# A third MLP product done as seven quarter products, fixed tiles for the raw up weights, and a rewritten passage from the up half to the down half

## The chip, the cores and the metric

The kernel runs on one core of a Trainium2 chip. The metric is the device time of one execution in microseconds (us), lower is better. All arithmetic that matters is float32: a matrix product is made of three TensorE passes over operands that were split into a high and a low part (`hi*hi + hi*lo + lo*hi`).

## The reference, cut to what matters

One decoder layer on x of shape (1, 1024, 1024): a first RMS norm, differential attention and a gated delta rule side by side, an output projection, and then the MLP, which is all that the change touches:

```
h = rms_norm(x, norm2_w)
x = x + jnp.square(jax.nn.relu(h @ w_up)) @ w_down      # w_up 1024 x 4096, w_down 4096 x 1024
```

Both products of the MLP are computed with a seven-product (Strassen-like) scheme: the operands are cut into 2 x 2 blocks, seven products of sums and differences of blocks take the place of eight products of blocks, and the blocks of the result are sums of the seven.

## The kernel before, in words

**The up half** (lines 2517 to 2871) makes `relu(h @ w_up)^2`. The 4096 hidden columns are cut into eight groups `g` of 512. In each group there are seven products, numbered 1 to 7. A whole product takes a weight block of 512 inputs x 256 columns and a block of 512 tokens: two column slices of 128 times four input slices times three passes, so 24 matmuls of 512 tokens each (`prod_up`, lines 2414 to 2416). For groups 2 to 7 the *second* product is cut once more: `sixth_second` does it as seven sub-products on quarters, each of two input slices times three passes on 256 tokens, so 42 matmuls of 256 (lines 2657 to 2659). Its results go to halves of the bank `Z` and VectorE adds them to the tile `ua` with `plus` (line 2632).

From group 2 on a group's work is six calls in a row, `sixth_second`, `first`, `third`, `seventh`, `fifth`, `fourth` (lines 2851 to 2862); `first` and `fifth` already do those products for the next group. PSUM holds the banks `X[0]`, `X[1]`, `Y`, `Z`. The raw weights of a group are four tiles `raw` named a, b, c, d, loaded by `load_w` (line 2534) into a pool of eight tiles; `combine` forms their sums and differences on VectorE (line 2568), `rounded` makes the high part on ScalarE (line 2572), `rest` the low part on VectorE (line 2576). The quarters of the weights for the second product are summed on GpSimd (`quarters`, lines 2584 to 2588) in the tile `qf`, which takes the place of tile `s4`, and split into `qs`.

A finished block of hidden values (tiles `ua`, `b`, `c`, `ud`, and the differences `s3`, `s4`) is written to one of seven DRAM buffers `ud1` to `ud7`, one for each product of the down half. `put` notes the transfer, and `flush(n)` issues all but the last `n` lists of noted transfers on SyncE (SP), whose transfers share one queue.

**The down half** (lines 2872 to 2996) does seven products in two passes `kg`, in the order 1, 5, 6, 3, 7, 2, 4. Each product has two halves. That makes 28 halves, numbered here m = 0 to 27, each of 48 matmuls of 512 columns (lines 2943 to 2945). A half needs 1 MB of hidden values (`u_raw(m)`: a load `ur<-ud` into one of the four tiles ur0 to ur3) and 1 MB of weights (`dn_raw`: two loads `dw` of 512 KB), both split into high and low parts by `split4`: casts on ScalarE (line 2293) and differences on VectorE (line 2294). For one half the order is two casts of `ur`, two of `dw`, each followed on VectorE by its difference. Finished banks are added to the accumulators `acc` by `leave` (line 2926).

Before, the tile of half m is `urs[max(m - 1, 0) % 4]`: halves 0 and 1 share ur0, half 3 has ur2, and half 4 is the first that has ur3. The tile ur3 lies in a pool that takes the place of the pools `up0` and `up1` (tiles `b`, `s4`, `ud`, `c`, `s3`), so its first load waits until the last writes out of `b` and `s4` have landed (lines 2963 to 2967).

TensorE's order is as written in the code throughout. From group 2 to the end of `first` of group 7 that of VectorE and ScalarE is as written too (lines 2849 to 2866); after that a scheduler sets it. SP's order is set by the scheduler in both kernels.

Of the kernel before, what the change touches and what calls it, by code (L numbers as in the profile page):

```python
# [9 lines left out]
F32 = mybir.dt.float32  # L10
# [8 lines left out]
P = 128  # L19
# [225 lines left out]
def tile_hymba_layer(  # L245
# [2273 lines left out]
    uctx = ctx.enter_context(ExitStack())  # L2519
    for name, cx, tags in (("ur0", tpctx, []), ("up1", uctx, ["b", "s4"]), ("up0", uctx, ["ud", "c", "s3"])):  # L2520
# [28 lines left out]
    def u_tile(g, n):  # L2549
        tag = f"ua{g % 2}" if n == "a" else "ud" if n == "d" else n  # L2550
        u[g][n] = ups[tag].tile([P, 2, 512], F32, tag=tag, name=tag, bufs=2 if n == "d" else 1)
        return u[g][n]
# [65 lines left out]

    Q_S = {}

    def quarters_w(g):
        raw = w[g]["b"]
        f = ups["s4"].tile([P, 4, 2, P], F32, tag="s4", name="qf", bufs=1)
# [4 lines left out]
        split([t[:, x].rearrange("p s k c -> p (s k c)") for x in range(2)], f.rearrange("p s k c -> p (s k c)"))  # L2628
        Q_S[g] = [[t[:, x, i] for x in range(2)] for i in range(4)]

# [8 lines left out]
    def slot(f, g):  # L2639
        puts.append([])  # L2640
        f(g)
        flush(2)

    def sixth_second(g):

        rest(g, 6)
        if g > 2:
            act2(u_tile(g - 1, "b"), X[(g - 1) % 2])
            put(g - 1, "b", 2)
        sw, o2 = Q_S.pop(g), early.pop((g, 2))  # L2650
        A = [[[x[:, 2 * j:2 * j + 2, i * P:i * P + P] for x in o2] for j in range(2)] for i in range(2)]
        a = u[g]["a"]
        r0, r1, z0, z1 = [Z[i // 2][:, i % 2 * 256:i % 2 * 256 + 256] for i in range(4)]

        def sub(out, wt, xt, start, stop):
            for k in range(2):
                T.matmul(out, wt[0][:, k], xt[0][:, k], start=start and k == 0, stop=False, skip_group_check=True)
                T.matmul(out, wt[0][:, k], xt[1][:, k], start=False, stop=False, skip_group_check=True)
                T.matmul(out, wt[1][:, k], xt[0][:, k], start=False, stop=stop and k == 1, skip_group_check=True)  # L2659

# [3 lines left out]
        plus(a[:, 0, 0:256], r0)  # L2664
        plus(a[:, 0, 0:256], r1)
        sub(z0, A[1][1], Q_T[3], True, True)
        sub(z1, sw[0], Q_T[0], False, False)
        plus(a[:, 1], Z[1])
        if g < NG - 1:
            rounded(g + 1, 1)  # L2670
        for _ in range(2):
# [9 lines left out]
        sub(z1, sw[3], B2[1][1], False, True)  # L2681
        if g < NG - 1:
            rest(g + 1, 1)
        combine(g, 3)
# [5 lines left out]
        rounded(g, 3)  # L2690

    def first(g):
        for _ in triples(g + 1, 1, X[1 - g % 2], True) if g < NG - 1 else ():
            pass
        S.copy(u_tile(g, "c"), X[g % 2])
        rest(g, 3)
        combine(g, 7)
        act2(u[g]["a"])
        put(g, "a", 1)
        rounded(g, 7)  # L2700

    def third(g):
        for _ in triples(g, 3, Y, False, True):
            pass
        S.copy(u_tile(g + 1, "a"), X[1 - g % 2])
        rest(g, 7)
        combine(g + 1, 5)
        rounded(g + 1, 5)

    def seventh(g):  # L2710
        t = u[g]
        for _ in triples(g, 7, X[g % 2]):
# [21 lines left out]
    def fourth(g):  # L2734
        t = u[g]
        for _ in triples(g, 4, X[g % 2], False, True):
            pass
        S.copy(u_tile(g + 1, "d"), Y)
        V.tensor_tensor(t["a"], t["c"], t["a"], ALU.subtract)
# [13 lines left out]
    def product(g, i):  # L2753
# [24 lines left out]
        elif i == 5:  # L2778
            S.copy(u_tile(g, "d"), Y)
        elif i == 6:  # L2780
# [6 lines left out]
        elif i == 7:  # L2787
# [3 lines left out]
            act2(t["d"])  # L2791
            put(g, "d", 4)
            V.tensor_tensor(t["c"], t["c"], t["d"], ALU.add)
# [35 lines left out]
    def loaded_after(g, i):  # L2829
        if i == 7:  # L2830
            load_w(g + 2, "ab")
        elif i == 4:
            load_w(g + 2, "cd")

    for g, i in todo:
        step(g, i)
        if (g, i) == (1, 6):
            quarters_x()
        elif (g, i) == (1, 3):
            sums = quarters_w(2)  # L2840
            next(sums)
        elif (g, i) == (2, 5):
            next(sums, None)
        loaded_after(g, i)
    rounded(2, 2)
    rest(2, 2)
    combine(2, 6)
    rounded(2, 6)
    ordered = ctx.enter_context(ExitStack())
    ordered.enter_context(tc.manual_schedule(engines={V.engine, S.engine}))  # L2850
    for g in range(2, NG - 1):
        slot(sixth_second, g)
        slot(first, g)
        slot(third, g)
        slot(seventh, g)
        sums = quarters_w(g + 1)
        next(sums)
        loaded_after(g, 7)
        slot(fifth, g)
        slot(fourth, g)  # L2860
        next(sums, None)
        loaded_after(g, 4)
    g = NG - 1
    slot(sixth_second, g)
    slot(first, g)
    ordered.close()
    step(g, 3)
    flush(1)
    rest(g, 7)
    step(g, 7)  # L2870
    step(g, 4)
    octx.close()

    ur = ctx.enter_context(tc.tile_pool(name="ur", bufs=1, **right))

# [5 lines left out]
    lo, hi = slice(0, 512), slice(512, 1024)  # L2881
    turn_of = [0]
    for tb in tiles:
        accs[tb] = row_tile("acc")

    ur0 = pools["ur0"].tile([P, 4, 512], F32, tag="ur0", name="ur0")
    urs = [ur0] + [ur.tile([P, 4, 512], F32, name=f"ur{i}") for i in (1, 2)]
    wds = [{} for _ in range(NK)]
# [14 lines left out]
    def u_raw(m):  # L2903
        if m < len(halves):
            kg, i, s = halves[m]
            g0 = 4 * kg + 2 * s
            return nc.sync.dma_start(urs[max(m - 1, 0) % 4].rearrange("p (g q) t -> p g q t", g=2),
                                     ud[i][g0:g0 + 2].rearrange("g p q t -> p g q t"))
# [8 lines left out]

    def down(kg, wd, i, flip, n, out, start, stop):
        bank = bankB if flip ^ (kg % 2) else bankA
# [10 lines left out]
        for s in range(2):  # L2930
            v = views[4 * (turn_of[0] % 2):][:4]
            turn_of[0] += 1
            m = halves.index((kg, i, s))
            raw = urs[max(m - 1, 0) % 4]
            split4(v[0:2], raw)
            split4(v[2:4], wd[n][s])
            u_raw(m + 4 if m else 1)
            seq = [(j, t) for t in (0, 2, 1, 3) for j in range(4)] if final and s else \
                [(j, t) for j in range(4) for t in range(4)]
            for j, t in seq:  # L2940
# [5 lines left out]
                if final and s1:  # L2946
                    leave(t)
        if not final:
            for t in range(4):
                leave(t)  # L2950

    u_raw(0)
    for n in "ab":
        for s in range(2):
            dn_raw(0, n, s)


    load_acc(tiles[:4])
    u_raw(2)
    u_raw(3)  # L2960
    for s in range(2):
# [10 lines left out]
    for kg in range(NK):  # L2972
# [5 lines left out]

        down(kg, wd, 1, 0, "a", (0, lo), True, False)
        both("b", "b", "a")  # L2980
        down(kg, wd, 5, 1, "b", (1, hi), True, False)
        both("b", "d", "b")
        down(kg, wd, 6, 0, "b", (0, hi), False, False)
        down(kg, wd, 3, 1, "d", (0, hi), False, True)
        both("a", "b", "a")
        down(kg, wd, 7, 0, "a", (1, hi), False, False)
        down(kg, wd, 2, 1, "c", (0, lo), True, True)
        if kg + 1 < NK:
            for s in range(2):
                dn_raw(kg + 1, "a", s)  # L2990
        both("b", "c", "b")
        down(kg, wd, 4, 0, "b", (1, lo), False, True)
        if kg + 1 < NK:
            for n in "bdc":
                for s in range(2):
                    dn_raw(kg + 1, n, s)
    manual.close()
# [48 lines left out]
```

## Time and profile before

| | |
|---|---|
| median of the runs before (lowest to highest, 3 runs) | 1190.36 us (1189.79 to 1192.09) |
| the profiled execution's own time | 1190.33 us |
| its span, first to last instruction | 1188.4 us |
| mean granted TensorE clock | 1.000 |
| busy: TensorE, VectorE, ScalarE, GpSimd | 1178.1, 878.1, 621.3, 190.1 us |
| up half from its steady part on, and down half | 666 to 880 us, and 880 to 1185 us |

In the profile's lines, a group names the code line, the engine, the operation and `out<-in` by tile names; buffer numbers are left out, so `ur<-ud` is any load of hidden values. "Idle before" is the engine's wait in front of the instruction, with what ended it. A transfer's "us to landing" runs from its issue on SP to its last byte. Matmuls are pipelined: one of 512 columns lasts 0.39 us from start to end, but the next one starts 0.23 us after it, so TensorE's pace is read from starts.

### The profile page before, as it was taken

Reading aid. Unit: us, or ns where it says so; the run is one execution under the profiler, and the core shown is the slowest. Engines: PE = TensorE matmul, PEld = TensorE weight load, DVE = VectorE, ACT = ScalarE, POOL = GpSimd, SP = SyncE. Lnnn points to the kernel's source line nnn. Section 1 sums busy time; section 2 is a strip of 40 time slices with the busy share of each in tenths; the row PEclk is TensorE's granted clock in tenths of the full one; section 3 lists DMA queues with packets and bytes.
Section 4 is the critical chain, followed back from the end, with each engine's and each line's share of the span. In section 5 each row is a group of like instructions: output and inputs, shape, how many; then the busy total and the mean of one; then the engine's idle time right before and its main releaser. Section 6 shows DMA issues by size and latency. Waiting matters only on the chain.

```text
span 1188.4 us, 17558 instructions
## 1 busy us (share of the span) xinstructions
PE 1178.1 (99%) x6196; PEld 988.8 (83%) x6196; DVE 878.1 (74%) x1648; ACT 621.3 (52%) x1141; POOL 190.1 (16%) x250
## 2 busy tenths in 40 slices
PE   9999999999999999999999999999999999999998
PEld 8988888788888788888888888888888888888887
DVE  7878799667778888886996666656689755786543
ACT  6656646344556765774765445445473333434330
POOL 2314211432222432222120000000000000000000
PEclk9999999999999999999999999999999999999999
DMA  9358644557545586344545444344399555422301
GB/s 355 121 133 197 183 116 98 127 181 209 188 151 171 153 216 162 90 88 152 178 154 186 177 156 160 127 157 177 143 338 379 204 193 213 142 81 96 142 36 71
DMA packets 179617, 196.09 MB, mean 165 GB/s; under 512 B 81529, under 2 KB 134313, under 8 KB 179529
## 3 DMA queue, kind: packets, MB, share of 16 engines
q1 hardware_dynamic: 173688, 181.56, 48.5%
q0 software_dynamic: 5696, 13.41, 3.5%
q8 instruction: 49, 0.80, 0.3%
q14 instruction: 40, 0.32, 0.1%
q10 hardware_dynamic: 144, 0.00, 0.0%
HBM read 132.73 MB, written 62.19 MB: 164 GB/s over the span
## 4 chain that ended last, share of the span: by engine, by line
PE 49%; DVE 1%; issue 0%; DMA 0%; ACT 0%; DVEq 0%
PE X L2416 5%; PE X L2415 5%; PE X L2414 5%; PE X L2943 4%; PE X L2944 4%; PE X L2945 4%; PE Y L2416 2%; PE Y L2415 2%; PE Y L2414 2%; PE Y L2943 2%; PE Z L2943 2%; PE Z L2944 2%; PE Y L2944 2%; PE Y L2945 2%; PE Z L2945 2%; PE Z L2659 1%
## 5 line engine op out<-in xcount | busy, mean ns | idle before, releaser
L2293 ACT CAST hH<-ur 128x1024 fp32r<-128x1024 f32 x56 | 58.6, 1051 | 167.6 <-PE Y L2944 89.4
L2294 DVE TENSOR_TENSOR hL<-ur,hH 128x1024 fp32r<-128x1024 f32 x56 | 68.2, 1222 | 78.1 <-ACT hH L2293 78.0
L2943 PE MATMUL X<-hH 128*128 128x512 f32 x224 | 87.1, 389 | 0.0
L2944 PE MATMUL X<-hL,hH 128*128 128x512 f32 x224 | 87.1, 389 | 0.0
L2945 PE MATMUL X<-hH,hL 128*128 128x512 f32 x224 | 87.1, 389 | 0.0
L2576 DVE TENSOR_TENSOR op<-raw,op 128x1024 fp32r<-128x1024 f32 x43 | 53.3, 1240 | 34.0 <-PE X L2415 25.0
L1228 PE MATMUL ps_dn<-hH,wH 128*128 128x512 f32 x192 | 76.5, 399 | 0.0
L1229 PE MATMUL ps_dn<-hL,wH 128*128 128x512 f32 x192 | 74.9, 390 | 0.0
L1230 PE MATMUL ps_dn<-hH,wL 128*128 128x512 f32 x192 | 74.9, 390 | 0.0
L2294 DVE TENSOR_TENSOR hL<-dw,hH 128x1024 fp32r<-128x1024 f32 x56 | 68.1, 1217 | 0.2 <-ACT hH L2293 0.2
L2572 ACT CAST op<-raw 128x1024 fp32r<-128x1024 f32 x43 | 44.9, 1043 | 38.5 <-PE Z L2659 23.6
L2293 ACT CAST hH<-dw 128x1024 fp32r<-128x1024 f32 x56 | 58.7, 1048 | 9.0 <-PE X L2945 4.4
L1835 ACT ACTIVATE pexp<-pexp,mx,small 128x128 f32<-128x128 f32 (+7 forms) x64 | 55.1, 862 | 12.5 <-DVE mx L1855 12.5
L829 DVE SCALAR_TENSOR_TENSOR cy<-cp,pv,cy 128x512 f32<-128x512 f32 x72 | 52.2, 736 | 9.8 <-ACT cy L826 9.2
L1334 ACT CAST wH<-wraw 128x512 fp32r<-128x512 f32 x66 | 40.5, 614 | 34.5 <-DMA wraw<-in_w_units_dram 18.5
L1713 PE MATMUL ps_qk<-hH,wH 128*128 128x512 f32 x128 | 53.7, 420 | 0.3 <-DVE tq L1628 0.3
L2165 PE MATMUL ps_op<-wH,hH 128*128 128x512 f32 x128 | 53.1, 415 | 0.0
L1336 DVE TENSOR_TENSOR wL<-wraw,wH 128x512 fp32r<-128x512 f32 x60 | 41.0, 683 | 13.4 <-ACT wH L1334 13.1
L1715 PE MATMUL ps_qk<-hH,wL 128*128 128x512 f32 x128 | 50.2, 392 | 0.0
L2167 PE MATMUL ps_op<-wH,hL 128*128 128x512 f32 x128 | 50.2, 392 | 0.0
L1714 PE MATMUL ps_qk<-hL,wH 128*128 128x512 f32 x128 | 50.0, 391 | 0.0
L2166 PE MATMUL ps_op<-wL,hH 128*128 128x512 f32 x128 | 50.0, 390 | 0.0
(449 smaller groups left out, 3512.6 us busy)
## 6 DMA issues: line engine op xcount, KB each, us to landing
ur<-ud SPq DMA_DIRECT2D x28, 1024.0 KB, 4.9
raw<-in_w_up_dram SPq DMA_DIRECT2D x32, 512.0 KB, 4.0
dw<-in_w_down_dram SPq DMA_DIRECT2D x32, 512.0 KB, 6.5
wraw<-in_w_units_dram SPq DMA_DIRECT2D x38, 256.0 KB, 4.1
ud<-ua SPq DMA_DIRECT2D x16, 512.0 KB, 5.9
ud<-s SPq DMA_DIRECT2D x16, 512.0 KB, 3.1
pka<-park_d SPq DMA_DIRECT2D x32, 192.0 KB, 4.1
xt<-in_x_dram SPq DMA_DIRECT2D x8, 512.0 KB, 10.2
```

What stands on the lines that cost most here:

```text
L1228: T.matmul(ps, wh[:, k, cs], hH[:, k, sl], start=(k == 0), stop=False)
L1229: T.matmul(ps, wh[:, k, cs], hL[:, k, sl], start=False, stop=False)
L1230: T.matmul(ps, wl[:, k, cs], hH[:, k, sl], start=False, stop=(k == KB - 1))
L1835: S.activation(e, e, AF.Exp, scale=negq[h][:, 8 * m + tb:8 * m + tb + 1], bias=bi[:, m:m + 1], accum_out=ssum[:, m:m + 1])
L2293: S.copy(dst[0], src)
L2294: V.tensor_tensor(dst[1], src, dst[0].bitcast(F32), ALU.subtract)
L2414: T.matmul(ps, op[0][:, k, cs], h[0][:, k, :], start=start and k == 0, stop=False, skip_group_check=True)
L2415: T.matmul(ps, op[0][:, k, cs], h[1][:, k, :], start=False, stop=False, skip_group_check=True)
L2416: T.matmul(ps, op[1][:, k, cs], h[0][:, k, :], start=False, stop=stop and k == 3, skip_group_check=True)
L2943: T.matmul(bank[t], v[0][:, j, sl], v[2][:, j], start=s0, stop=False, skip_group_check=True)
L2944: T.matmul(bank[t], v[0][:, j, sl], v[3][:, j], start=False, stop=False, skip_group_check=True)
L2945: T.matmul(bank[t], v[1][:, j, sl], v[2][:, j], start=False, stop=s1, skip_group_check=True)
```

## The change

- **Third product in quarters, groups 3 to 7.** `third_quarters` replaces 24 matmuls of 512 by 42 of 256, on halves of `Z` and on `Y`. Weight quarters come from a second `quarters_w(g, True)` (GpSimd sums in the place of tile `s3`, one more cast, one more difference); quarters of the tokens are made once in group 2 (`quarters_x3` on GpSimd, `operand_x3`). VectorE gets four more additions into `c` (`plus` in `third_quarters` and `spread`).
- **Raw weights in six fixed tiles.** `load_w` writes a group's tile into the one that the group before (a, b) or the one before that (c, d) had; the loads of a, b, c, d are issued at four places instead of two. Tile `ud` has one buffer instead of two, and the copy out of `Y` into it moves from `fourth` to `sixth_second`.
- **The passage and the down half.** The last group's third, seventh and fourth product are written out by hand with the first splits of the down half between them (`ready`), and VectorE and ScalarE follow the written order to the end (`ordered.close()` is now last). A half's operands are prepared one half ahead (`upcoming(m + 1)`), and the additions to `acc` are held back by half a product (`behind`). The tile of half m is now `urs[m % 4]`: half 0 has ur0, half 1 ur1, half 2 ur2, and half 3 is the first that has ur3.

The core of the diff (`...` marks what is left out):

```diff
-                t = row_tile("raw").rearrange("p (k c) -> p k c", k=4)
+                back = 1 if n in "ab" else 2
+                t = w[g - back][n] if g - back > 1 else row_tile("raw").rearrange("p (k c) -> p k c", k=4)
...
+    def third_quarters(g):
+        last = g == NG - 1
+        sw, A, c = Q_S3.pop(g), quartered(early.pop((g, 3))), u[g]["c"]
+        r, z = Z[0][:, 0:256], Z[1][:, 0:256]
...
+        sub(r, A[0][0], B3[0][0], True, False)
+        plus(c[:, 0, 0:256], r)
...
+        sub(z, sw[0], Q_T3[0], True, True)
+        if not last:
+            twice()
+        if not last:
+            sub(Y[:, 0, 0:256], A[0][1], B3[1][0], False, True)
+            S.copy(u_tile(g + 1, "a"), X[1 - g % 2])
+        rest(g, 7)
+        sub(r, sw[1], Q_T3[1], False, False)
+        plus(c[:, 0, 256:512], r)
...
+            sub(Y[:, 1, 0:256], A[1][1], Q_T3[3], False, True)
+        sub(Y[:, 0, 256:512], sw[3], B3[1][1], False, True)
...
+        sub(r, sw[2], Q_T3[2], False, True)
...
     def u_raw(m):
...
-            return nc.sync.dma_start(urs[max(m - 1, 0) % 4].rearrange("p (g q) t -> p g q t", g=2),
+            return nc.sync.dma_start(urs[m % 4].rearrange("p (g q) t -> p g q t", g=2),
...
+    def upcoming(m):
+        if 1 < m < len(halves):
+            kg, i, s = halves[m]
+            v = views[4 * (m % 2):][:4]
+            split4(v[0:2], urs[m % 4])
+            split4(v[2:4], wds[kg][NAMES[i]][s])
+            u_raw(m + 4)
...
     flush(0)
     uctx.close()
     pools["uc"] = tpctx.enter_context(tc.tile_pool(name="uc", bufs=1, **left))
     urs.append(pools["uc"].tile([P, 4, 512], F32, name="ur3"))
-    last = u_raw(4)
+    last = u_raw(3)
+    u_raw(5)
     with tc.issue_after(last.ins):
         load_acc(tiles[4:])
```

**SP at the end of the passage.** The issues around the last write `ud3<-s4` stand on SP before as follows (`ud5` is read by halves 2 and 3, `ud6` by 4 and 5, `ud3` by 6 and 7, and `ur0` to `ur3` are the four tiles):

```order
L2907 DMA ur2_9385<-ud5_128 128x2x1024
L2899 DMA dw_9405<-in_w_down_dram 128x2x512 x2
L2899 DMA dw_9408<-in_w_down_dram 128x2x512
L2562 DMA ud4_127<-ud_9167 128x1024
L2907 DMA ur0_9383<-ud6_129 128x2x1024
L2562 DMA ud2_125<-b_9330 128x1024
L2562 DMA ud5_128<-c_9261 128x1024
L2562 DMA ud6_129<-ua1_9061 128x1024
L2907 DMA ur1_9384<-ud3_126 128x2x1024
L2562 DMA ud3_126<-s4_9367 128x1024
L2907 DMA ur2_9385<-ud3_126 128x2x1024
L2907 DMA ur3_9421<-ud6_129 128x2x1024
```

And in the changed kernel, from the load of half 2 on:

```order
L3007 DMA ur2_9552<-ud5_128 128x2x1024
L2999 DMA dw_9576<-in_w_down_dram 128x2x512
L2563 DMA ud5_128<-c_9393 128x1024
L2999 DMA dw_9576<-in_w_down_dram 128x2x512
L3007 DMA ur0_9449<-ud6_129 128x2x1024
L2999 DMA dw_9579<-in_w_down_dram 128x2x512
L2563 DMA ud6_129<-ua1_9157 128x1024
L3007 DMA ur1_9551<-ud6_129 128x2x1024
L2563 DMA ud2_125<-b_9495 128x1024
L2563 DMA ud3_126<-s4_9569 128x1024
L3007 DMA ur2_9552<-ud3_126 128x2x1024
L3007 DMA ur3_9589<-ud5_128 128x2x1024
```

Before, the load that is last here and waits for the write of `s4` brings half 4, and the first row brings half 3. Now the first row brings half 2, and the last one half 3.

**ScalarE in the first halves of the down half.** Before, from the splits of half 1 on (the casts of `ur0` at the top are half 1, those of `ur1` half 2):

```order
L2293 CAST hH_131<-ur0_9383 128x2x512 x2
L2790 COPY b_9330<-X1_7225 128x1024
L2465 ACTIVATE ud_9167<-ud_9167 128x1024
L2466 ACTIVATE ud_9167<-ud_9167 128x1024
L2465 ACTIVATE b_9330<-b_9330 128x1024
L2466 ACTIVATE b_9330<-b_9330 128x1024
L2293 CAST hH_131<-dw_9393 128x2x512
L2293 CAST hH_131<-ur1_9384 128x2x512 x2
```

Now, from the splits of half 0 on (`ur1` is half 1, `ur2` half 2, `ur3` half 3):

```order
L2293 CAST hH_131<-ur0_9449 128x2x512
L2293 CAST hH_131<-dw_9454 128x2x512 x2
L2293 CAST hH_131<-ur1_9551 128x2x512 x2
L2465 ACTIVATE b_9495<-b_9495 128x1024
L2466 ACTIVATE b_9495<-b_9495 128x1024
L2293 CAST hH_131<-ur2_9552 128x2x512 x2
L2293 CAST hH_131<-dw_9512 128x2x512 x2
L2293 CAST hH_131<-ur3_9589 128x2x512 x2
L2293 CAST hH_131<-dw_9515 128x2x512 x2
```

The casts now come two and two, `ur` ahead of `dw`; the last activation of `b`, from which `s4` is made, stands behind the casts of half 1.

**VectorE in the third product of group 3.** Before, from the low part of product 7's weights to the difference `s3`:

```order
L2576 TENSOR_TENSOR op_8224<-raw_7829,op_8223 128x1024
L2568 TENSOR_TENSOR raw_8101<-raw_8101,raw_8103 128x1024
L2632 TENSOR_TENSOR c_8217<-c_8217,Y_6811 128x1024
L2576 TENSOR_TENSOR op_8256<-raw_8101,op_8255 128x1024
L2718 TENSOR_TENSOR s3_8291<-ua1_7983,c_8217 128x1024
```

Now the same stretch, with the low part of the weight quarters (`qs`) ahead:

```order
L2657 TENSOR_TENSOR qs_8144<-qf_8139,qs_8144 128x1024
L2661 TENSOR_TENSOR c_8236<-c_8236,Z0_7290 128x256
L2661 TENSOR_TENSOR c_8236<-c_8236,Z1_7291 128x2x256
L2577 TENSOR_TENSOR op_8245<-raw_7825,op_8244 128x1024
L2661 TENSOR_TENSOR c_8236<-c_8236,Z0_7290 128x256
L2569 TENSOR_TENSOR raw_7600<-raw_7600,raw_7602 128x1024
L2661 TENSOR_TENSOR c_8236<-c_8236,Z0_7290 128x512
L2661 TENSOR_TENSOR c_8236<-c_8236,Y_6811 128x1024
L2577 TENSOR_TENSOR op_8293<-raw_7600,op_8292 128x1024
L2813 TENSOR_TENSOR s3_8336<-ua1_7990,c_8236 128x1024
```

Four additions out of `Z` and the difference of `qs` are new in this stretch.

More of the change, by code (lines that the diff above doesn't have):

```diff
@@ L2642, in slot, with sub, quartered @@
         flush(2)
+    def sub(out, wt, xt, start, stop):
+        for k in range(2):
+            T.matmul(out, wt[0][:, k], xt[0][:, k], start=start and k == 0, stop=False, skip_group_check=True)
+            T.matmul(out, wt[0][:, k], xt[1][:, k], start=False, stop=False, skip_group_check=True)
+            T.matmul(out, wt[1][:, k], xt[0][:, k], start=False, stop=stop and k == 1, skip_group_check=True)
+    def quartered(o):
+        return [[[x[:, 2 * j:2 * j + 2, i * P:i * P + P] for x in o] for j in range(2)] for i in range(2)]
     def sixth_second(g):
         rest(g, 6)
+        last = g == NG - 1
         if g > 2:
@@ L2649, in sixth_second @@
             put(g - 1, "b", 2)
+        S.copy(u_tile(g, "d"), Y)
         sw, o2 = Q_S.pop(g), early.pop((g, 2))
-        A = [[[x[:, 2 * j:2 * j + 2, i * P:i * P + P] for x in o2] for j in range(2)] for i in range(2)]
+        A = quartered(o2)
         a = u[g]["a"]
         r0, r1, z0, z1 = [Z[i // 2][:, i % 2 * 256:i % 2 * 256 + 256] for i in range(4)]
[L2655 to L2659, printed above, removed]
         steps = triples(g, 6, X[g % 2])
@@ L2694, in first @@
             pass
+        if g == NG - 1:
+            for _ in sums_w3.pop():
+                pass
+            S.copy(u_tile(g, "c"), X[g % 2])
+            rounded(g, 7)
+            act2(u[g]["a"])
+            put(g, "a", 1)
+            return
         S.copy(u_tile(g, "c"), X[g % 2])
         rest(g, 3)
+        if g > 2:
+            next(sums_w3[0])
         combine(g, 7)
+        if g > 2:
+            next(sums_w3.pop(), None)
         act2(u[g]["a"])
@@ L2865, in tile_hymba_layer @@
     slot(first, g)
[L2866 to L2874, printed above, removed]
+    slot(third, g)
     bankA = Z + [Y[:, 0], Y[:, 1]]
@@ L2881, in tile_hymba_layer @@
     lo, hi = slice(0, 512), slice(512, 1024)
-    turn_of = [0]
-    for tb in tiles:
-        accs[tb] = row_tile("acc")
     ur0 = pools["ur0"].tile([P, 4, 512], F32, tag="ur0", name="ur0")
-    urs = [ur0] + [ur.tile([P, 4, 512], F32, name=f"ur{i}") for i in (1, 2)]
+    urs = [ur0]
     wds = [{} for _ in range(NK)]
@@ L2916, in split4, with ready, down @@
             split([x[:, j:j + 2] for x in dst], src[:, j:j + 2])
-    def down(kg, wd, i, flip, n, out, start, stop):
+    def ready(s, weights, j):
+        v = views[4 * s:][:4]
+        dst, src = (v[2:4], wds[0]["a"][s]) if weights else (v[0:2], urs[s])
+        split([x[:, j:j + 2] for x in dst], src[:, j:j + 2])
+    def down(kg, i, flip, out, start, stop, then=None):
         bank = bankB if flip ^ (kg % 2) else bankA
```

217 lines of the change are left out of this document (164 added, 53 removed).

## The prediction

> **What bounds the kernel now.** I read the page's busy shares first, then the list of TensorE's waits, then busy time by stage.
>
> ```profile
> PE 1178.1 (99%) x6196; PEld 988.8 (83%) x6196; DVE 878.1 (74%) x1648; ACT 621.3 (52%) x1141; POOL 190.1 (16%) x250
> ```
>
> ```profile
> PE ps_w L567 <- POOL ident masks.py:199: 1.5, 1, 1.5
> ...
> PE ps_r L528 <- ACT dg L523: 0.2, 1, 0.2
> ```
>
> ```profile
> 0.00:603.00 603.00, 596.59 (x3516) 503.02 (x3517) 488.36 (x1277) 361.45 (x877) 166.55 (x224) 1.00 0.58 162
> 603.00:630.00 27.00, 26.92 (x120) 21.95 (x119) 26.64 (x32) 20.88 (x26) 6.19 (x2) 1.00 0.68 225
> ...
> 704.00:742.00 38.00, 38.00 (x191) 32.31 (x190) 24.85 (x26) 19.41 (x21) 2.86 (x4) 1.00 0.44 153
> ...
> 856.00:880.00 24.00, 24.00 (x115) 20.15 (x114) 19.06 (x19) 15.14 (x16) 0.00 (x0) 1.00 0.81 288
> 880.00:1032.00 152.00, 152.00 (x672) 125.91 (x671) 108.83 (x97) 59.89 (x60) 0.00 (x0) 1.00 0.65 242
> ```
>
> The list has eleven waits of TensorE, none of them at a line of the MLP. From 630 us on its busy time equals the stretch. So in everything that the change touches TensorE is the bound, at a granted clock of 1.00: a matmul that goes shortens the kernel by its pace, work on other engines costs nothing while it stays hidden, and a new wait of TensorE costs its full length, since nothing behind it can catch up. There is no wait to win here. Pace is read from starts:
>
> ```profile
> 664.21 0.28 PE L2657 MATMUL Z<-hH,op 128*128 128x256 f32 x1
> ...
> 667.08 0.40 PE L2414 MATMUL X<-T0h,op 128*128 128x512 f32 x1
> ...
> 674.75 0.39 PE L2414 MATMUL X<-hH,op 128*128 128x512 f32 x1
> ...
> 680.19 0.39 PE L2414 MATMUL Y<-hH,op 128*128 128x512 f32 x1
> ```
>
> The first 24 quarter matmuls of the second product take 667.08 - 664.21 = 2.87 us, 119.6 ns each. A whole product's 24 take 680.19 - 674.75 = 5.44 us, 226.7 ns each.
>
> **Third product in quarters.** It removes 24 x 226.7 ns = 5.44 us and adds 42 x 119.6 ns = 5.02 us: 0.42 us less per group, 2.1 us less over groups 3 to 7, all of it on the bound. Between 256 and 512 columns the trace shows no gap worth a term.
>
> What comes with it lies on other engines:
>
> ```profile
> L2632 DVE TENSOR_TENSOR ua<-ua,Z 128x256 f32<-128x256 f32 x24 | 10.1, 421 | 6.1 <-PE Z L2659 5.4
> L2632 DVE TENSOR_TENSOR ua<-ua,Z 128x512 f32<-128x512 f32 x12 | 8.2, 687 | 5.2 <-PE Z L2659 5.2
> L2294 DVE TENSOR_TENSOR qs<-qf,qs 128x1024 fp32r<-128x1024 f32 x6 | 7.3, 1224 | 6.6 <-ACT qs L2293 6.6
> L2584 POOL TENSOR_TENSOR qf<-raw 128x256 f32<-128x256 f32 x6 | 4.6, 764 | 190.5 <-DMA ud<-s 190.5
> L2611 POOL COPY qr<-qr 128x512 f32<-128x512 f32 x2 | 6.2, 3119 | 29.4 <-issue 29.4
> ...
> L2293 ACT CAST hH<-ur 128x1024 fp32r<-128x1024 f32 x56 | 58.6, 1051 | 167.6 <-PE Y L2944 89.4
> ```
>
> VectorE gets, per group, two additions of 256 (0.42 each), two of 512 (0.69 each) and one difference of 1024 (1.22): 3.4 us on top of 24.85 of 38. ScalarE gets a cast of 1.05 us on top of 19.41, GpSimd four sums of 0.76 on top of 2.86. All three have room, so the sum is nought on average. The tight place is the half bank `r`: its second sub-product may start only when `c` has taken the first, and between the two TensorE has 12 quarter matmuls, 1.43 us, against an addition of 0.42; if VectorE has more than 1 us of other work in front there, TensorE waits for the excess. I take 0; the first rival below takes it up. The eight sums of token quarters in group 2 (512 elements on GpSimd) are not in the trace: bounded by 0.76 for half as many elements and by the 3.1 us of a GpSimd copy of that size, nearest to twice 0.76, about 1.5 each and 12 in all. They are needed a whole group, 38 us, later: 0, and still 0 at 3.1 each.
>
> **Six fixed raw tiles, one `ud` tile.** A load now waits for the last reader of the same tile, and on SP later issues queue behind it. Each has at least one call (5.4 us for a whole product) between issue and first use; VectorE is the one to wait, then TensorE. The copy out of `Y` moves to the next call and waits for the write of the tile; `Y` is next written two calls later. I take 0 for these, at most some tenths.
>
> **The passage.** Here a new wait appears. In the changed kernel half 3 is the first in ur3, whose first load waits until the last write of `s4` has landed; before, that was half 4. So the load is needed 48 matmuls, 10.9 us, earlier. How it stood before:
>
> ```profile
> 861.58 0.37 SPq L2907 DMA_DIRECT2D ur<-ud  x1
> ...
> 896.60 0.32 SPq L2562 DMA_DIRECT2D ud<-s  x1
> ```
>
> ```profile
> 863.42 0.38 SPq L2899 DMA_DIRECT2D dw<-in_w_down_dram  x1
> ```
>
> ```profile
> ud<-s SPq DMA_DIRECT2D x1, 512.0 KB, 12.5
> ```
>
> ```profile
> 909.22 0.37 SPq L2907 DMA_DIRECT2D ur<-ud  x1
> ```
>
> ```profile
> ur<-ud SPq DMA_DIRECT2D x1, 1024.0 KB, 5.3
> ```
>
> ```profile
> 863.00:878.00 15.00, 15.00 (x68) 12.38 (x67) 11.86 (x12) 12.62 (x13) 0.00 (x0) 1.00 0.95 334
> 878.00:893.00 15.00, 15.00 (x68) 12.43 (x67) 15.00 (x12) 11.18 (x11) 0.00 (x0) 1.00 1.02 376
> 893.00:909.00 16.00, 16.00 (x72) 13.27 (x71) 15.18 (x14) 5.06 (x5) 0.00 (x0) 1.00 0.92 355
> ```
>
> The transfers are full from 863 to 909 us (share 0.92 to 1.02). The write of `s4`, issued at 896.60, landed 12.5 us later, at 909.1; at 909.22 the first load of ur3 went out and landed 5.3 later, at 914.5. From the issue of half 0 at 861.58 to that landing SP's order counts six `ur` of 1 MB, twelve `dw` and seven writes of 512 KB: 31 units of 512 KB in 47.5 us, 1.53 us each.
>
> In the changed order the stretch up to the landing of `s4` begins with the first `dw` and has five `ur`, twelve `dw`, seven writes: 29 units, 44.4 us. That first `dw` waits for the end of product 6 of group 7, which comes four groups' savings earlier, 1.7 us: 863.42 - 1.7 = 861.7. So `s4` lands at 906.1, and half 3, with 1 MB (half 6) ahead of it in SP's order, as another load had then, at 906.1 + 0.1 + 5.3 = 911.5.
>
> TensorE's first matmul of the down half:
>
> ```profile
> 879.79 0.39 PE L2943 MATMUL Z<-hH 128*128 128x512 f32 x1
> ```
>
> Now 879.79 - 2.1 = 877.7, and half 3 is due three halves of 48 x 226.7 ns = 10.88 later, at 910.3. Its operands after the landing:
>
> ```profile
> 914.57 2.00 ACT L2293 CAST hH<-ur 128x1024 fp32r<-128x1024 f32 x2 [0.83 <-DMA ur<-ud]
> ```
>
> ```profile
> 915.66 2.36 DVE L2294 TENSOR_TENSOR hL<-ur,hH 128x1024 fp32r<-128x1024 f32 x2 [0.45 <-ACT hH L2293]
> ```
>
> The first matmul needs the third cast (two of `ur`, one of `dw`), 2.0 + 1.05 = 3.0 us after the landing, the second one the third difference: 1.1 us behind the first cast's start, then 2.36 for two and 1.2 for the third, 4.6 us. So the second matmul starts at 911.5 + 4.6 = 916.1 in place of 910.55: **TensorE waits 5.5 us** in front of and in half 3. Twenty-four halves follow at TensorE's pace and give none of it back. Nor does it matter if an earlier half is late by a fraction: the landing, not TensorE, sets this end. Halves 0 to 2 come out ready by the same count: half 0 is the 7th unit (861.7 + 7 x 1.53 = 872.4, due 877.7), half 1 is the 14th unit (861.7 + 14 x 1.53 = 883.1, due 888.6), half 2 the 18th (889.2, due 899.5).
>
> The unknown is the pace of the transfers. At the best of the three stretches throughout (376 GB/s against a mean of 355) the 44.4 us become 41.9 and the wait 3.0; at the worst (334) they become 47.2 and the wait 8.3. I take the mean, which is this same stretch with almost the same transfers.
>
> [...]
>
> The rest of the down half (preparing one half ahead, holding back the additions to `acc`, differences of weights earlier) changes no matmul and hides behind a TensorE that never waited there: 0. The end, one addition and a last write behind the last matmul, is the same.
>
> **The sum**, against the profiled execution's 1190.33 us, practically the median of 1190.36: 1190.33 - 2.1 + 5.5 = **1193.7 us**. About 0.2%, 2.4 us, is what a measurement of this kernel can tell from no change; so slower means above 1192.7, faster below 1188.0.
>
> **Rivals.**
>
> *VectorE or GpSimd become late within a group.* For it: 28.3 us of some 37.3 would be taken on VectorE, the order is fixed, and GpSimd's sums now meet it twice per group. One difference that met them took longer:
>
> ```profile
> 708.60 1.22 DVE L2568 TENSOR_TENSOR raw<-raw 128x1024 f32<-128x1024 f32 x1
> ...
> 712.53 1.60 DVE L2576 TENSOR_TENSOR op<-raw,op 128x1024 fp32r<-128x1024 f32 x1 [1.22 <-PE X L2415]
> ```
>
> 1.60 us against 1.22. Against it: that cost TensorE nothing. It decides once VectorE is over 1 us late at `c += r`; half a microsecond per group would be 2.5 us more, 1196.2. [...] Chance 0.10.
>
> *The load of half 3 comes in time.* The other side: it decides at the landing of half 3. If that is 3.4 us earlier (29 units in 41 us, 385 GB/s), the wait shrinks to the 2.1 us saved and the time is that of before; at 5.6 us earlier there is no wait, and the time is 1190.33 - 2.1 = 1188.2. For it: single stretches reached 376, and the mix has fewer `dw` waiting behind a late issue; against it: the mean over 46 us was 355. Chance 0.28, within it 0.09 for under 1188.0 (a slightly larger saving is enough) and 0.19 for no change.
>
> *The forecast*, a wait of 3.5 to 8 us at half 3: chance 0.62; in 0.13 of it the wait is under 4.5 us and the sum within 0.2%, in 0.49 it is slower.
>
> **How the numbers follow.** Slower 0.49 + 0.10 = 0.59, same 0.13 + 0.19 = 0.32, faster 0.09. The forecast's own range is 1191.7 to 1196.2; the range reaches down to 1188.4, nearly to the case without a wait, which leaves out about 0.1 at each end: 1188.4 to 1196.2.
>
> **What would show it.** In the profile after: 42 matmuls of 256 per third product in about 5.0 us and group to group 37.25 us instead of the 37.67 that six whole products and 42 quarter matmuls make at these paces; the first matmul of the down half near 877.7 us; then TensorE's first wait of the MLP at about 910 us, released by ScalarE and VectorE (casts of `ur`), behind a load `ur<-ud` that ScalarE waits for; the write of `s4` landing near 906 and that load near 911.5. The prediction is wrong if half 3 starts without a wait, if the wait stands at another half or inside the groups, or if quarter matmuls in the third product run at another pace than 0.12 us.

## The result and the profile after

The changed kernel takes **1198.15 us** (median of 6 runs, 1197.03 to 1198.61), the kernel before in the same session 1190.72 us (6 runs, 1189.79 to 1192.09): ratio 1.006, 95% interval 1.0047 to 1.0073. It is slower, as forecast, but by 7.4 us instead of 3.3. The profiled execution took 1198.07 us with a span of 1196.4 us, 8.0 more than before.

The waits of TensorE in the changed kernel, those at a line of the MLP (us in total, times, longest):

```profile
PE X L3043 <- ACT hH L2293: 4.6, 1, 4.6
...
PE X L3044 <- DVE hL L2294: 0.8, 1, 0.8
...
PE Z L3045 <- DVE hL L2294: 0.5, 1, 0.5
```

Before there was none. All three stand in the down half (lines 3043 to 3045 are its matmuls), none inside the groups. Busy time by stretch, with the granted clock in the third column from the end:

```profile
704.00:742.00 38.00, 38.00 (x211) 33.15 (x210) 29.27 (x33) 20.63 (x21) 7.71 (x8) 1.00 0.43 153
...
911.00:919.00 8.00, 2.51 (x7) 1.45 (x6) 4.43 (x4) 5.51 (x6) 0.00 (x0) 0.83 1.02 407
919.00:923.00 4.00, 4.00 (x11) 3.03 (x11) 4.00 (x3) 1.78 (x3) 0.00 (x0) 0.50 1.02 322
```

In the groups (first row) TensorE stays busy all the time, with VectorE at 29.27 of 38 us instead of 24.85. The row to stop at is the last. From 919 to 923 us TensorE is busy all the time, but begins 10 matmuls in 4 us instead of 18 (the row's 11 counts the one that was still running at 919), and the granted clock is 0.50. A list of waits doesn't show this: a slow matmul is busy. TensorE's own timeline, with the passage to half 0, then the last matmul of half 2 and what follows it (start, length, line; idle before):

```profile
877.66 0.39 PE L2416 MATMUL X<-T2h,op 128*128 128x512 f32 x1
878.09 0.50 PE L3043 MATMUL Z<-hH 128*128 128x512 f32 x1
878.43 0.40 PE L3044 MATMUL Z<-hL,hH 128*128 128x512 f32 x1
879.35 0.50 PE L3045 MATMUL Z<-hH,hL 128*128 128x512 f32 x1 [0.52 <-DVE hL L2294]
879.69 0.40 PE L3043 MATMUL Z<-hH 128*128 128x512 f32 x1
...
911.44 0.39 PE L3045 MATMUL X<-hH,hL 128*128 128x512 f32 x1
916.48 0.79 PE L3043 MATMUL X<-hH 128*128 128x512 f32 x1 [4.65 <-ACT hH L2293]
918.12 0.80 PE L3044 MATMUL X<-hL,hH 128*128 128x512 f32 x1 [0.84 <-DVE hL L2294]
918.71 0.63 PE L3045 MATMUL X<-hH,hL 128*128 128x512 f32 x1
919.14 0.63 PE L3043 MATMUL X<-hH 128*128 128x512 f32 x1
...
923.27 0.40 PE L3044 MATMUL X<-hL,hH 128*128 128x512 f32 x1
```

Against the normal spacing of 0.227 us, these starts give the sum. The last matmul of the up half begins at 877.66 and the first of the down half starts 0.20 late; the three gaps behind it are 0.11, 0.69 and 0.11 too long: half 0 costs 1.1 us. In front of half 3 the gap of 5.04 is 4.81 too long, the next one of 1.64 is 1.41 too long: the wait costs 6.2 us. From 918.12 to 923.27 there are 12 spacings in 5.15 us, where 2.72 would be normal: the slow stretch costs 2.4 us.

The up half gained. From the first quarter matmul of group 2 to the first matmul of the down half it was 879.79 - 664.21 = 215.58 us before. Now that quarter matmul starts at

```profile
663.89 0.28 PE L2675 MATMUL Z<-hH,op 128*128 128x256 f32 x1
```

and the down half could have begun at 877.66 + 0.23 = 877.89, 214.0 us later: 1.6 us less. With 0.3 us from an earlier start at 663.89 the sum is -0.3 - 1.6 + 1.1 + 6.2 + 2.4 = +7.8 us. The last matmul started at 1184.20 us before and 1192.11 after, +7.9:

```profile
1184.20 0.39 PE L2945 MATMUL X<-hH,hL 128*128 128x512 f32 x1
```

```profile
1192.11 0.39 PE L3045 MATMUL X<-hH,hL 128*128 128x512 f32 x1
```

What half 3 waited for, on SyncE's queue and then on ScalarE:

```profile
893.57 0.33 SPq L2563 DMA_DIRECT2D ud<-s  x1
...
907.79 0.37 SPq L3007 DMA_DIRECT2D ur<-ud  x1
```

```profile
913.49 1.99 ACT L2293 CAST hH<-ur 128x1024 fp32r<-128x1024 f32 x2 [16.81 <-DMA ur<-ud]
```

The write of `s4` goes out at 893.57. The first load of ur3, which needs its landing, goes out at 907.79, and ScalarE, idle for 16.8 us, starts its casts at 913.49. That is the chain of the forecast, with the landing some 1.6 us and the cast 2.0 us later than it said.

### The profile page after: what moved, and what is told of

The parts are those of the page before. It is cut to its first block, busy times and chain, and to the rows that moved or that the text cites. A ratio compares the mean times of both kernels' runs of the same rounds, so it can differ in the third digit from the quotient of the medians.

```text
span 1196.4 us, 17818 instructions
## 1 busy us (share of the span) xinstructions
PE 1180.5 (99%) x6286; PEld 992.9 (83%) x6286; DVE 899.9 (75%) x1677; ACT 628.4 (53%) x1150; POOL 232.9 (19%) x278
## 4 chain that ended last, share of the span: by engine, by line
PE 79%; DVE 8%; DMA 7%; issue 2%; SPq 2%; ACT 2%; POOL 1%; DVEq 0%; ACTq 0%; POOLq 0%
PE X L2414 5%; PE X L2416 5%; PE X L2415 5%; PE X L3044 4%; PE X L3045 4%; PE X L3043 4%; PE ps_o L2010 3%; PE ps_sc L1889 2%; PE ps_op L2167 2%; PE ps_op L2165 2%; PE ps_op L2166 2%; PE Y L2416 2%; PE ps_qk L1713 2%; PE Y L2414 2%; PE Y L3044 2%
## 5 line engine op out<-in xcount | busy, mean ns | idle before, releaser
L2577 DVE TENSOR_TENSOR op<-raw,op 128x1024 fp32r<-128x1024 f32 x44 | 57.9, 1317 | 21.1 <-PE X L2415 16.0
L2293 ACT CAST hH<-dw 128x1024 fp32r<-128x1024 f32 x56 | 55.9, 1045 | 6.4 <-DMA dw<-in_w_down_dram 3.8
L3043 PEld LDWEIGHTS X<-hH 128*128 128x128 f32 x224 | 42.7, 191 | 14.0 <-ACT hH L2293 5.1
L3044 PEld LDWEIGHTS X<-hL,hH 128*128 128x128 f32 x224 | 42.6, 190 | 10.2 <-DVE hL L2294 1.3
```

The costliest lines, as they stand in the source:

```text
L2293: S.copy(dst[0], src)
L3043: T.matmul(bank[t], v[0][:, j, sl], v[2][:, j], start=s0, stop=False, skip_group_check=True)
L3044: T.matmul(bank[t], v[0][:, j, sl], v[3][:, j], start=False, stop=False, skip_group_check=True)
```

## The experiments

The theory after the result: the loss is half 3's late load (ur3 one half earlier), plus the half clock behind the wait, plus a late half 0, less what the quarters save. Rival A: the quarters cost, by what they put on VectorE and GpSimd. Rival B: the order now set for VectorE and ScalarE costs. Rival C: the passage moves too much, whichever tile is used. Times are medians; each ratio is to the kernel before in the same session, whose median was 1190.28 us for the first four kernels and 1189.93 us for the last four.

### Half 3 in another tile

```diff
-            return nc.sync.dma_start(urs[m % 4]...
+            return nc.sync.dma_start(urs[m if m < 3 else (m - 3) % 4]...
...
-    u_raw(4)
+    u_raw(3)
...
-    last = u_raw(3)
-    u_raw(5)
+    last = u_raw(6)
+    u_raw(4)
```

> The changed kernel with another tile for four halves: half 3 gets ur0 (in the place of half 4's load on SyncE's queue), half 4 ur1, half 5 ur2, and half 6 is the first in ur3; everything else as in the changed kernel. Theory (half 3's load behind the landing of the write of s4, plus TensorE at half the granted clock for some 7 us afterwards, 2.5 us by the spacing of the matmuls there): half 3's load lands near 900 us as half 4's did, the waits of 4.8 and 1.4 us and the slow stretch go, and the time is 1198.15 - 6.2 - 2.5 = 1189.4 us. Rival A (the loss comes from the quarters and what they put on VectorE and GpSimd in the groups) and rival B (from the rewritten order of VectorE and ScalarE in the down half): the tile changes neither, so the time stays near 1198. Rival C (too many bytes in the passage, whichever tile): a wait of some microseconds moves to another half, 1194 or more.

Measured: 1190.07 us, ratio 0.9994 (0.9985 to 1.0002). Its waits of TensorE in the MLP, and the casts of half 3 on ScalarE:

```profile
PE Z L3043 <- ACT hH L2293: 1.0, 1, 1.0
...
PE Z L3045 <- DVE hL L2294: 0.5, 1, 0.5
```

```profile
901.12 1.06 ACT L2293 CAST hH<-ur 128x1024 fp32r<-128x1024 f32 x1 [2.35 <-DMA ur<-ud]
```

Both waits are at bank `Z` in half 0; those at `X` are gone, with half 3's operand on ScalarE at 901 us instead of 913. Against the kernel before of its own session this kernel is 0.2 us faster where the changed kernel is 7.4 us slower, so one tile number is worth 7.6 us here, with the quarters and the written order unchanged. So A and B do not explain the loss, and C does not either, since the same megabytes move. What is left of the time over the theory's 1189.4 is half 0, which is later in this trace than in the changed kernel's (2.1 us instead of 1.1).

### The tile of half 3 alone, in the kernel before

```diff
-            return nc.sync.dma_start(urs[max(m - 1, 0) % 4]...
+            return nc.sync.dma_start(urs[m % 4]...
...
-            u_raw(m + 4 if m else 1)
+            u_raw(m + 4)
...
-    u_raw(2)
-    u_raw(3)
+    u_raw(1)
+    u_raw(2)
...
-    last = u_raw(4)
+    last = u_raw(3)
```

> The kernel before with one part of the change alone, the tile of half m being urs[m % 4], so that half 3 is the first in ur3 and half 1 has ur1; no quarters in the third product, no raw tiles fixed, no order set in the down half. Theory: the wait in front of half 3 appears here too, 4 to 6 us, and the clock falls behind it where TensorE idles for about 4 us or longer at a stretch: 1190.7 + 4 to 8.5 = 1194.7 to 1199 us. Rival A or B (quarters or the written order make the loss): 1190.7, no change.

Measured: 1199.06 us, ratio 1.0068 (1.0056 to 1.0080), 8.8 us slower: as much as the whole loss, without any other part of the change. TensorE's timeline at half 3, and the stretch behind it:

```profile
913.96 0.39 PE L2945 MATMUL X<-hH,hL 128*128 128x512 f32 x1
917.21 0.50 PE L2943 MATMUL X<-hH 128*128 128x512 f32 x1 [2.86 <-ACT hH L2293]
...
918.85 0.80 PE L2945 MATMUL X<-hH,hL 128*128 128x512 f32 x1 [0.75 <-DVE hL L2294]
```

```profile
918.00:924.00 6.00, 5.25 (x13) 4.09 (x13) 4.22 (x3) 0.10 (x1) 0.00 (x0) 0.50 1.03 376
```

A gap of 3.25 us, one of 1.30 (from 917.55, left out here), and then 0.50 as granted clock: behind a gap 3.0 us too long the clock fell as it did behind 4.8. The 4 us or longer of the expectation was the author's estimate; no run shows a limit there. The two waits and the slow stretch make some 7 us; half 1, which has another tile here too, is late by another 1.3.

### The wait filled with matmuls

Repeated matmuls behind half 2 keep TensorE at work; 20 of them, or 8.

```diff
+            for _ in range(20 if m == 2 else 0):
+                T.matmul(bank[3], v[0][:, 3, sl], v[2][:, 3], start=False, stop=False, skip_group_check=True)
```

> The changed kernel with 20 more matmuls of 512 columns behind those of half 2: they repeat its last product into the same bank, so the output holds that product more than once. They last 20 x 0.227 = 4.5 us and lie in the wait of 4.8 us in front of half 3, so that TensorE idles there for some 0.5 us instead of 5.0; half 3's load and its landing stay. Theory (2.5 us of the loss is the granted clock that falls to a half after the long wait): the clock stays at 1.00 over 916 to 924 us and the time falls by 2.5 to 1195.6 us although TensorE does more. Rival (the slow matmuls after the wait come from late operands or from transfers beside them): the time stays at 1198.1 us.

Measured: 1195.21 us, ratio 1.0041 (1.0029 to 1.0053). The same two stretches as above:

```profile
911.00:919.00 8.00, 7.51 (x33) 5.92 (x32) 4.34 (x4) 5.42 (x6) 0.00 (x0) 1.00 1.02 408
919.00:923.00 4.00, 4.00 (x19) 3.33 (x18) 4.00 (x3) 1.79 (x3) 0.00 (x0) 1.00 0.97 332
```

With 20 matmuls more the kernel is 2.5 us faster (4.9 us slower than the kernel before of its session, instead of 7.4), the clock stays at 1.00 and the second row counts 19 matmuls where it counted 11. Transfers and casts are as late as in the changed kernel: the DMA share is 1.02 and 0.97 in these rows, and half 3's first cast starts at 913.58 instead of 913.49. So the slow matmuls came from the clock, not from late operands or from transfers beside them.

> As the kernel with 20 repeated matmuls behind half 2, with 8 of them: 1.8 us of the wait are filled, and TensorE idles some 3.2 us at a stretch in front of half 3 and 1 us behind its second matmul. Theory (the clock falls behind a wait of this kind): open on which side 3.2 us lies, since the kernel before with the new tiles fell to a half behind 3.0 us in this place and the one with halves 5 and 6 later did not behind 0.6 and 1.1: 1198 if it falls, 1195.5 if it does not; in no case more than 1198.2, as the filler lies in the wait. Rival (late operands make the slow matmuls): 1198.1 in any case.

Measured: 1196.51 us, ratio 1.0055 (1.0042 to 1.0069), between the two values that were expected. In the profiled execution, the fastest of six with 1194.75 us, the gap in front of half 3 is shorter than expected, as half 3's operands came earlier:

```profile
911.03 1.75 PE L3049 MATMUL X<-hH 128*128 128x512 f32 x7
914.01 0.50 PE L3043 MATMUL X<-hH 128*128 128x512 f32 x1 [1.23 <-ACT hH L2293]
915.65 0.80 PE L3044 MATMUL X<-hL,hH 128*128 128x512 f32 x1 [1.14 <-DVE hL L2294]
916.25 0.63 PE L3045 MATMUL X<-hH,hL 128*128 128x512 f32 x1
```

The first row is the last seven repeated matmuls. They end at 912.78 us, so the last of them starts at 912.39; the 1.62 us from there to 914.01 are 1.4 too long, and so are the 1.64 behind it, and the clock falls nevertheless: the lengths of 0.63 are those of the half clock above. Full speed came back at 919.08, earlier than in the changed kernel.

### Halves 5 and 6 loaded behind half 3

```diff
     last = u_raw(3)
-    u_raw(5)
     with tc.issue_after(last.ins):
+        u_raw(5)
...
-            u_raw(m + 4)
+            if m == 2:
+                with tc.issue_after(last.ins):
+                    u_raw(6)
+            else:
+                u_raw(m + 4)
```

> The changed kernel with the loads of halves 5 and 6 issued behind that of half 3 instead of ahead of it: 2 MB less stand in front of the landing of s4 and of half 3. Theory: at 1.5 us for 512 KB, a part of it beside work that waits anyway, half 3 lands some 4 us earlier, and TensorE's two waits together fall from 6.2 to about 2 us; so short a wait leaves the granted clock at 1.00, and the 2.5 us behind it go too: 1198.15 - 4.2 - 2.5 = 1191.5 us. Rival without the clock (2.5 us are lost in half 3 in any case): 1194. Rival A and rival B (quarters, or the order of VectorE and ScalarE): no change, 1198.

Measured: 1192.46 us, ratio 1.0020 (1.0011 to 1.0029), nearer to the theory's 1191.5 than to the rival's 1194, though single runs reach both. Half 3 in its profile:

```profile
912.50 0.39 PE L3045 MATMUL X<-hH,hL 128*128 128x512 f32 x1
913.21 0.50 PE L3043 MATMUL X<-hH 128*128 128x512 f32 x1 [0.33 <-ACT hH L2293]
914.85 0.50 PE L3044 MATMUL X<-hL,hH 128*128 128x512 f32 x1 [1.13 <-DVE hL L2294]
915.18 0.39 PE L3045 MATMUL X<-hH,hL 128*128 128x512 f32 x1
```

The two waits are 0.48 and 1.41 us, 1.9 together instead of 6.2, and the matmuls behind them keep their 0.39. It was not so in every execution: over eleven runs the mean granted clock lies between 0.997 and 1.000 and the time between 1189.60 and 1196.07 us, while all six runs of the changed kernel have 0.997 or 0.998 and all five with 20 repeated matmuls 1.000. The clock is not all of this spread: one run with 1.000 took 1193.92 us and one with 0.997 took 1193.00.

### A longer wait

The tiles of before inside the changed kernel, which makes half 1 late instead of half 3:

```diff
-            return nc.sync.dma_start(urs[m % 4]...
+            return nc.sync.dma_start(urs[max(m - 1, 0) % 4]...
...
-    u_raw(4)
+    u_raw(1)
...
-    u_raw(1)
+    u_raw(2)
...
-    u_raw(2)
+    u_raw(3)
...
-    last = u_raw(3)
+    last = u_raw(4)
```

> The changed kernel with the tiles of before (halves 0 and 1 share ur0, half 3 in ur2, half 4 first in ur3), which puts the load of half 1 behind those of halves 2 and 3 and three loads of weights on SyncE's queue. Theory: half 3 no longer waits, but half 1 does, some 10 to 12 us (its load is the 21st transfer of the passage instead of the 14th, 1.5 us each), and behind so much longer a wait the slow clock costs the same 2.5 to 3 us as behind 4.8, since it comes back after some microseconds of work whatever the wait was: 1188.2 + 11 + 2.5 = 1202, 1200 to 1205 us. Rival (the slow stretch grows with the wait): 5 us or more for it, 1205 or more. Rival A or B (not the tile): 1198.

Measured: 1203.20 us, ratio 1.0109 (1.0096 to 1.0122). At half 1:

```profile
890.65 0.39 PE L3045 MATMUL Y<-hH,hL 128*128 128x512 f32 x1
900.74 0.80 PE L3043 MATMUL Z<-hH 128*128 128x512 f32 x1 [9.71 <-ACT hH L2293]
...
905.49 0.39 PE L3044 MATMUL Y<-hL,hH 128*128 128x512 f32 x1
```

The gap is 9.9 us too long, twice the changed kernel's. From 900.74 to 905.49 there are 10 spacings in 4.75 us, 2.5 us more than normal. So the slow clock cost as much behind a wait twice as long: 2.5 us here, 2.4 in the changed kernel.

### Third product whole again

`third` runs the whole product for all groups, and the weight quarters, their split and their additions go. The token quarters of group 2 are still written, one of them over a block of h that the whole product reads, so the output is not the reference's.

```diff
     def third(g):
-        if g > 2:
-            third_quarters(g)
-            return
         for _ in triples(g, 3, Y, False, True):
             pass
+        if g == NG - 1:
+            rest(g, 7)
+            return
```

> The changed kernel with the third product of groups 3 to 7 whole again (the weight quarters, their cast and difference and the additions out of Z gone too; the token quarters are still made in group 2 and not used); raw tiles, passage and down half as in the changed kernel. Theory: the up half lasts 2.1 us longer, half 0's load goes out earlier, since ur0 is no longer held by weight quarters, and is in time; the wait in front of half 3 and the slow clock stay, since the landing of the write of s4 moves with the up half: about 1198.15 + 2.1 - 1.1 = 1199.2 us, 1198 to 1200. Rival A (the quarters are what costs): 1190 or less. Rival B (the written order of the down half): also 1199 to 1200, so that this run doesn't speak on it.

Measured: 1198.38 us, ratio 1.0072 (1.0059 to 1.0085), inside what the theory gave, but not by its parts:

```profile
890.18 0.39 PE L3037 MATMUL Y<-hH,hL 128*128 128x512 f32 x1
891.66 0.50 PE L3035 MATMUL Z<-hH 128*128 128x512 f32 x1 [1.09 <-ACT hH L2293]
...
892.92 0.50 PE L3037 MATMUL Z<-hH,hL 128*128 128x512 f32 x1 [0.53 <-DVE hL L2294]
...
894.03 0.63 PE L3037 MATMUL Z<-hH,hL 128*128 128x512 f32 x1
...
917.38 0.50 PE L3035 MATMUL X<-hH 128*128 128x512 f32 x1 [1.23 <-ACT hH L2293]
919.02 0.50 PE L3036 MATMUL X<-hL,hH 128*128 128x512 f32 x1 [1.14 <-DVE hL L2294]
919.35 0.40 PE L3037 MATMUL X<-hH,hL 128*128 128x512 f32 x1
```

Half 0 is in time here, as expected. Half 1 is not: gaps 1.25 and 0.69 us too long, and behind them the half clock. SP's order, which a scheduler sets, has the load of half 1 behind the writes of `ud` and `s3` here and ahead of them in the changed kernel; it goes out at 881.53 us instead of 878.33. Half 3 waits only 1.4 + 1.4 us, and behind that the clock did not fall, though the same pair of waits brought it down in the kernel with 8 repeated matmuls. The time is that of the changed kernel though the up half is longer by 1.6 us, so the quarters are not what costs; but with half 1 late as well this run is no clean removal of the quarters, and the next one says more.

### No tile waited for, with the quarters

Half 0 is loaded into two raw tiles of group 6 that nothing reads any more, half 1 gets ur0, half 2 ur1, half 3 ur2, and half 4 is the first in ur3.

```diff
+    first_half = [w[NG - 2][n].rearrange("p (q k) c -> p q (k c)", q=2) for n in "cd"]
...
+            if m == 0:
+                for j in range(2):
+                    nc.sync.dma_start(first_half[j], ud[i][g0 + j])
+                return
-            return nc.sync.dma_start(urs[m % 4]...
+            return nc.sync.dma_start(urs[max(m - 1, 0) % 4]...
```

> Quarters and everything else as in the changed kernel, but no tile is waited for: half 0 is loaded early into the two raw tiles of group 6 that nothing reads any more (c and d), half 1 then has ur0 and goes out in the place of half 0's load, half 2 ur1, half 3 ur2, half 4 ur3, and so on as before. Theory: with both late operands gone (half 3, and half 0, whose load of ur0 waited for the weight quarters there) what is left is the saving of the quarters, 2.1 us: 1190.3 - 2.1 = 1188.2 us, with TensorE busy from 860 us to the end. Rival (the quarters save nothing, their 2.1 us go to gaps elsewhere): 1190.3. Rival B (the written order costs in the down half): above 1190.

Measured: 1189.15 us, ratio 0.9991 (0.9983 to 1.0000), midway between the theory's 1188.2 and the rival's 1190.3, so the trace has to tell them apart. TensorE's first quarter matmul, first matmul of the down half and last matmul, and its busy time where the others waited:

```profile
664.95 0.28 PE L2675 MATMUL Z<-hH,op 128*128 128x256 f32 x1
...
878.84 0.39 PE L3048 MATMUL Z<-hH 128*128 128x512 f32 x1
...
1183.26 0.39 PE L3050 MATMUL X<-hH,hL 128*128 128x512 f32 x1
```

```profile
880.00:940.00 60.00, 60.00 (x266) 49.71 (x265) 47.18 (x41) 27.34 (x28) 0.00 (x0) 1.00 0.88 339
```

TensorE never waits in the MLP. The up half from the first quarter matmul on takes 878.84 - 664.95 = 213.89 us, 1.7 less than before; the down half from first to last start 304.42 us, against 1184.20 - 879.79 = 304.41 before. So the written order of VectorE and ScalarE costs nothing (B), and the quarters save 1.7 us (A is wrong in sign). Between the medians there are 0.8 us. In the traces the missing 0.7 lies ahead of the change: the first quarter matmul starts at 664.95 here and at 664.21 before, and in the other traces anywhere from 662.75 to 664.84. Each against its own kernel before, this kernel is 8.2 us faster than the changed one; against the kernel before the gain is at the edge of what a measurement can tell.

## Why the prediction was wrong, point by point

**Direction, place and chain were right.** TensorE is the bound, the only long wait is in front of half 3, its cause is the first load of ur3 behind the landing of `s4`. The experiment with another tile removes it, and the tile alone in the kernel before produces it. By the prediction's own sign (a wait at another half) the short wait at half 0 still counts against it.

**The step that failed** is "a new wait of TensorE costs its full length, since nothing behind it can catch up". The long waits cost more than their length, because the matmuls behind them ran at half the granted clock: 2.4 us in the changed kernel, 2.5 behind a wait of 9.9, and nothing with the wait filled. The trace of before held no row for it, since TensorE has no long wait there in the MLP and its clock stands at 1.00; the prediction read that 1.00 as a property of the kernel, in a trace where TensorE's longest wait is 1.5 us. The length of a wait alone doesn't tell whether the clock falls: it fell behind waits of 4.8 and 9.9 us, and it fell too behind 1.25 and 0.69 us with two matmuls between them (figures at the end).

**The wait itself** was sized 5.5 and measured 6.2 us. Half 3's first cast came at 913.49 instead of 911.5, the transfers from the first `dw` (861.86) to the landing of `s4` (907.8) taking 45.9 us instead of 44.4; half 3 was due at 911.7 instead of 910.3, which gave part of it back.

**"Halves 0 to 2 come out ready by the same count"** failed for half 0. The count of transfers put its landing at 872.4. Its load went out only here, and its cast waited for it:

```profile
867.17 0.37 SPq L3007 DMA_DIRECT2D ur<-ud  x1
```

```profile
876.99 1.05 ACT L2293 CAST hH<-ur 128x1024 fp32r<-128x1024 f32 x1 [0.58 <-DMA ur<-ud]
```

The tile ur0 is taken by the weight quarters `qs` of group 7's third product, which the change itself added, and is free when that product's last matmul has read them. That matmul ends at 867.14 us, just ahead of the load:

```profile
866.86 0.28 PE L2677 MATMUL Z<-hH,qs 128*128 128x256 f32 x1
```

The prediction counted bytes ahead of the load, and did not ask what held its tile. Cost: 1.1 us here, and 2.1 in the trace with half 3 in another tile, where it was the only wait left. With half 0 in other tiles it is gone.

**The quarters** were sized at 2.1 us and save 1.6 to 1.7. From first quarter matmul to first quarter matmul a group took 739.69 - 701.95 = 37.74 us before and takes 776.48 - 739.12 = 37.36 in the changed kernel where nothing disturbs it, so 0.38 less instead of 0.42. In two of the four full groups 0.1 us more is lost where the last sub-product of the third product begins: there one quarter matmul follows the one before after 0.23 instead of 0.12 us. What holds it up was not tried.

**The rivals.** VectorE or GpSimd late within a group: at most these tenths, with TensorE never listed as waiting there; no run shows the half microsecond per group that the prediction put on it. The load in time: not so, though the pace was at times higher than the 355 GB/s that the prediction took as the mean: the stretch from 911 to 919 us moved 407. The sum without the failed terms would have been 1190.33 - 1.6 + 6.2 = 1194.9; the two that were missing, 2.4 and 1.1, make it 1198.4 against 1198.07.

## What to carry to other kernels

Where TensorE never stops, price a new wait of some microseconds as its length plus the slow clock that can follow it (1.6 to 2.7 us in the five traces where it did), and look at the granted clock by stretch, since the list of waits doesn't show it. When a change gives tiles new tenants, ask of each early load what last reads the tile that it goes to, those readers included that the change adds. And a wait that is set by a landing is best removed by another tile, not by fewer bytes: one tile number gave back 7.6 us here, 2 MB less in front of it some 5, each against the kernel before of its own session.

## What the runs showed of the hardware

- The granted clock fell to 0.50 behind waits much shorter than 3 us as well: it did behind 1.25 + 0.69 us, it did in one trace and did not in another behind 1.4 + 1.4 us, and in eleven runs of one kernel (1.9 us in the one traced) the mean clock differed from run to run, between 0.997 and 1.000. What decides beside the length was not shown.
- The time at 0.50 differed from trace to trace. Read in stretches of 0.2 us, it lasted 6.8 us in the changed kernel and in the kernel before with the new tiles, 10.2 with half 1 late (5.6 of it before TensorE went on), and 3.4 both with 8 repeated matmuls and at half 1 of the kernel with the third product whole. The longer ones are twice and three times the shortest; the cause was not tried.
- Full speed came back between 4.7 us (wait of 9.9) and 7.3 us (wait of 3.0) after the first matmul behind the wait, and 6.6 us after it in the changed kernel (wait of 4.8); the longest wait did not make it later.
- Three of GpSimd's four sums of weight quarters became slower when each group had eight of them instead of four (0.74 us before, 1.07 to 1.28 now; the first kept its 0.77). One of them in the changed kernel, and then before:

```profile
L2588 POOL TENSOR_TENSOR qf<-qf,raw 128x256 f32<-128x256 f32 x11 | 14.0, 1277 | 0.0
```

```profile
L2587 POOL TENSOR_TENSOR qf<-qf,raw 128x256 f32<-128x256 f32 x6 | 4.4, 735 | 0.0
```

It cost TensorE nothing, and its cause was not tried.
